# A hybrid GLA and Fourier diffusion step on one core: earlier copies of the folded h, one modulation half on TensorE, 12 Fourier units in the output gates

## The chip, the cores and the metric

The kernel runs as one launch on one core of a Trainium2 chip. The metric is the device time of a launch in microseconds (us). The profile names the engines PE (TensorE, with PEld for its weight loads), DVE (VectorE), ACT (ScalarE), POOL (GpSimd) and SP (SyncE, which here only issues transfers). All arithmetic is float32. PE gets its products at that precision by splitting each operand in a high part (a rounded copy) and a low part (the rest), and adding three products: high x high, high x low, low x high.

## The reference

There are 384 tokens (128 context, 256 latent) of width 2048, and one layer. Cut to what matters:

```python
mod = silu(cond) @ w_ada + b_ada            # six rows of 2048: sh1 sc1 ga1 sh2 sc2 ga2
h = rmsnorm(x) * (1 + sc1) + sh1
q, k, v, g, lr_f, lr_b, fo = split(h @ w_in)
o = rms(gla_forward(q, k, v) + gla_backward(q, k, v)) * silu(g)
f = fft2(fo, axes=(position, channel of a group)).real
g_a, g_b = split(sigmoid(h @ w_gate + b_gate))
m = (g_a * (o @ w_br_gla) + g_b * (f @ w_br_four)) @ w_out
x = x + ga1 * rmsnorm(m)
h = rmsnorm(x) * (1 + sc2) + sh2
x = x + ga2 * rmsnorm((silu(h @ w_ffn_gate) * (h @ w_ffn_up)) @ w_ffn_down)
```

Outputs are x of both token groups and the final GLA states.

## The kernel before, in words

Everything is held transposed: 128 channels on the partitions, the 384 tokens along the free axis. The order of PE, ACT, DVE and POOL is the order in which the program is written; SP's is set by a scheduler. A 512 KB weight goes through `load` (a transfer into a tile `raw`) and `split` (ACT rounds it to `whi`, DVE subtracts to `wlo`); `grab` takes a split weight that is ready and splits the one that comes next, so that DVE and ACT run about three weights ahead of PE. `proj` makes one 128 x 384 output from two weights, a half of 24 matmuls each, and calls a side generator behind each half.

The stages, in order:
- **Modulated input, v, q, k, decay.** h is built (tiles `A_hi`, `A_lo`), v and the other columns of w_in are projected.
- **Merge gates with GLA beside them.** 25 of the 32 column blocks of w_gate; the results go to DRAM (`gates_d`).
- **Folding** (`run_after`, 14 turns). A turn is one projection half of the last seven gate blocks, and a table `after` lists what follows it. `ends(n)` adds h's parts (`t`) and forms sums and differences of mirrored positions (`r`, `over_ends`); `parts(n)`, one turn later, splits r into high and low (`hF`, `over_parts`); `f` multiplies hF by a weight of w_in that was itself folded (`fold_across`, L248 and L249), on PE at L998 and L999 (`pfo`). Turns 2 to 9 have one such product, turns 10 to 13 two. In this stage up to five weights are loaded ahead (`depth`), three of them into extra tiles `raw3`.
- **Output gates with the transform beside them.** Eight blocks `("o", i)` of w_in; `gcol` transposes GLA's output (`pt`), applies the gate (`gs`) and splits it. The side generator runs the rest of the Fourier transform (`dft`), which reads a table of constants `cd` (L1051).
- **Merge.** Sixteen `("a", i)` blocks of w_br_gla, with the gates and the Fourier results read back from DRAM. Sixteen Fourier units (`four`, L1185 and L1186: 33 matmuls with a weight of w_br_four, then sums, a gate, and a store to `four_d`) are spread over these two stages by `mix_order`, `BF` of them among the output gates.
- **Output projection** (`wout`), with the norm's sums beside it, and then the **feed-forward** part.

Rows three to five of the modulation (m = 2, 3, 4, in two halves each) are made in the background by `ada_rest`: 16 steps per half, each of which loads 512 KB of w_ada (`adaw`, on POOL's queue) and adds it, scaled by the conditioning of each token group, to `adacc` on DVE (L679, two operations per step). Eight small matmuls (L687) and two transposes finish a half. `next(ada)` makes one step; the list of places where it stands, and the factor `rate[0]` in the output projection, spread the steps.

Of the kernel before, what the change touches and what calls it, by code (L numbers as in the profile page):

```python
# [11 lines left out]
F32 = mybir.dt.float32  # L12
# [8 lines left out]
P = 128  # L21
# [15 lines left out]
G = 1024  # L37
XU = 2
GF = 25
BF = 10  # L40
GD = 256


# [64 lines left out]
def tile_step(ctx: ExitStack, tc: tile.TileContext, a, o):  # L108
# [77 lines left out]
        mix_order += [("o", i)] + [("b", next(fourier)) for _ in range(BF * (i - 1) // 6 - BF * (i - 2) // 6)]  # L186
    for i in range(KT):
        mix_order.append(("a", i))
        if i in (1, 2, 4, 6, 8, 10):
            mix_order.append(("b", next(fourier)))  # L190
    folded = set()
    for b, i in mix_order:
# [25 lines left out]
    def load(raw=None):  # L218
        n, src = next(srcs, (0, None))
        if src is not None:  # L220
            spare = spare_raws.pop() if raw is None and spare_raws else None
            if spare:
                raw = spare.tile([P, G], F32, tag="raw3", name="raw3", bufs=3)
            elif raw is None:
                raw = wp.tile([P, G], F32, tag="raw", name="raw", bufs=2)
            dst = raw if len(src.shape) == 2 else raw.rearrange("p (n x) -> p n x", n=src.shape[1])
            SP.dma_start(dst, src)
            raws.append((raw, 1 if n in folded else 2 if n in across else 0, spare))
# [134 lines left out]
    def split_act(hi, lo, src):  # L363
        ACT.copy(hi, src)
        DVE.tensor_sub(lo, src, hi.bitcast(F32))  # L365
# [303 lines left out]
    def ada_rest(todo):  # L669
        for m, half in todo:  # L670
# [19 lines left out]
                    )  # L690
            yield from ada_tail(pr, m, half)

    def over_ends(k, t, r):

        DVE.tensor_add(t, *(x[:, k : k + 2, :].bitcast(F32) for x in hT))
        ACT.copy(r[:, :, 0 : HC + 1 : HC], t[:, :, 0 : TC + 1 : TC])
        for lo, n, e in ((0, TC, 0), (TC, TL, HC)):
            h, o = n // 2, HT + (0 if lo == 0 else HC - 2)
            hi = lo + n - 1
            DVE.tensor_add(r[:, :, e + 1 : e + 1 + h], t[:, :, lo + 1 : lo + 1 + h], t[:, :, hi : hi - h : -1])  # L700
            DVE.tensor_sub(r[:, :, o : o + h - 1], t[:, :, lo + 1 : lo + h], t[:, :, hi : hi - h + 1 : -1])

    def over_parts(k, r):

        x = hF[k // 4]
        split_act(*(x[:, k % 4 : k % 4 + 2, n, :] for n in range(2)), r)


    gates_d = dram.tile([32, P, T], F32, name="gates_d")
# [4 lines left out]
        return qk[:, h:8:4, t * P : (t + 1) * P]  # L714

    rate = [1.0]
    ada_gen = ada_rest([(m, half) for m in (2, 3, 4) for half in range(2)])
    ada = paced(ada_gen, rate)
    with ExitStack() as s:
        pg = s.enter_context(tc.tile_pool(name="pg", bufs=1))  # L720
# [243 lines left out]
    def nyq_load(eng, h):  # L964
        for g in range(4):
            src = a["w_br_four"][8 * h : 8 * h + 8, 32 * g : 32 * g + 1, (2 * g + 1) * P : (2 * g + 2) * P]
            eng.dma_start(
                wr[g : g + 65 : 32, :].rearrange("p (i c) -> p i c", c=P),
                src.rearrange("i p c -> p i c").to_broadcast([3, 8, P]),
            )  # L970

    nyq_load(POOL, 0)
    with ExitStack() as s:
        more = s.enter_context(tc.tile_pool(name="more", bufs=1))
        hF = [actp.tile([P, 4, 2, T], F32R, tag=t, name="hF") for t in ("C_lo", "B_hi", "B_lo")]
        hF.append(more.tile([P, 4, 2, T], F32R, tag="hF", name="hF"))
        spare_raws.extend([more] * 3)
        depth[0] = 5
        sums, folds = [], {}

        def ends(n):
            t, r = (more.tile([P, 2, T], F32, tag=z, name=z) for z in ("t", "r"))
            over_ends(2 * n, t, r)
            folds[n] = r

        def across_n(h, n):
            if n == 0:
                sums[:] = [pss.tile([P, 2, hi - lo], F32, tag="side", name="pfo") for _ in range(2) for lo, hi, _ in parts]
            w = take()
            push()  # L990
            w_of = [x.rearrange("p (g i k c) -> p i k g c", g=2, i=2, k=2) for x in w]
            for k in range(2):
                kt = 2 * n + k
                x = hF[kt // 4][:, kt % 4]
                for g in range(2):
                    for i, (lo, hi, _) in enumerate(parts):
                        p = sums[2 * g + i]
                        PE.matmul(p, w_of[0][:, i, k, g, :], x[:, :, lo:hi], start=kt == 0, stop=False)  # L998
                        PE.matmul(p[:, 0], w_of[1][:, i, k, g, :], x[:, 0, lo:hi], start=False, stop=kt == KT - 1)  # L999
            if n == 7:  # L1000
                for g in range(2):
                    X.append(px.tile([P, T], F32, tag="yb", name="X", bufs=4))
                    for i, (lo, hi, _) in enumerate(parts):
                        p = sums[2 * g + i]
                        ACT.copy(X[-1][:, lo:hi], p[:, 1])
                        DVE.tensor_add(X[-1][:, lo:hi], X[-1][:, lo:hi], p[:, 0])

        def run_after():
            for at, todo in enumerate(after):
                for what, *n in todo:  # L1010
                    if what == "ends":
                        ends(*n)
                    elif what == "parts":
                        over_parts(2 * n[0], folds.pop(n[0]))
                    else:
                        if n == [1, 5]:
                            depth[0] = 2
                            spare_raws.clear()
                        across_n(*n)
                if at in (0, 1, 11, 13):  # L1020
                    next(ada, None)
                yield

        ra = run_after()
        for i in range(GF, 32):
            proj(psm, hT, gate(more, i), ra)
        catch_up()
        depth[0] = 0
        xq = px.tile([P, HT], F32, name="xq")
        POOL.memset(xq, 0.0)  # L1030
        qb = pss.tile([P, HT], F32, tag="side", name="pfq")
        for kb in range(0, KT, 4):
            for x_ in range(2):
                for k in range(kb, kb + 4):
                    q = 32 * (k % 4)
                    PE.matmul(
                        qb[q : q + 4, :], wq[:, k, :], hF[k // 4][:, k % 4, x_, 0:HT].bitcast(F32),
                        start=kb == 0 and x_ == 0, stop=kb == KT - 4 and x_ == 1,
                    )
        for q in range(0, P, 32):  # L1040
            ACT.copy(xq[q : q + 4, :], qb[q : q + 4, :])
# [3 lines left out]
    with ExitStack() as s:  # L1045
# [1 line left out]
        fold_in.append(pc)  # L1047
        pw = 448
        d2 = pc.tile([P, 2 * pw], F32R, name="d2")
        cd = pc.tile([P, NC - C_CE], F32, name="cd")  # L1050
        SP.dma_start(cd, a["consts"][:, C_CE:NC])  # L1051
        table = lambda at, n, rows=P: cd[0:rows, at - C_CE : at - C_CE + n]


# [60 lines left out]
        def nyq_weights():  # L1115

            n = D // 2
            for h in range(2):
                if h:
                    nyq_load(SP, 1)  # L1120
                    yield
                    yield
                w = wn[:, n * h : n * h + n]
                ACT.copy(w, wr)
                DVE.tensor_sub(w[32:64], wr[32:64], w[32:64].bitcast(F32))
                yield

        df = dft()

        nw = nyq_weights()  # L1130

        def side():
            while True:
                next(ada, None)
                next(df, None)
                next(nw, None)
                yield
# [66 lines left out]
        for b, i in mix_order:  # L1204
            if b == "o":
                if i == 1:
                    gate_of()
                proj(psm, hT, lambda p, i=i: gcol(p, i), sd)
                if i == 1:
                    gate_of()  # L1210
                continue
            if b == "b":
                for g in (df, nw):
                    for _ in g:
                        pass
                four(i)
            else:
                catch_up()
                if mT is None:
                    mT = alloc_A()  # L1220
                if i >= KT - 6:
                    next(ada, None)
                p = psm.tile([P, T], F32, tag="mm", name="pmm")
                gemm(p, grab(hold=True), oT, 8)
                g, y = gates.pop((b, i))
                DVE.tensor_mul(g, g, p)
                DVE.tensor_add(y, y, g)
                settle()
                if late:
                    split_act(*late.pop())  # L1230
                late.append((mT[0][:, i, :], mT[1][:, i, :], y))
            gate_of()
# [7 lines left out]
    with ExitStack() as s:  # L1240
# [42 lines left out]
            ACT.activation(sq2, mg32(i), AF.Square)  # L1283
            return sq0, pr, sq2

        rate[0] = 0.75
        spare_h = {-4: ((pe, "hid_hi", 1), (pe, "hid_lo", 1)), -2: ((pe, "S0", 1), (pe, "S1", 1))}
        spare_w = ((adap, "adaw", 2), (adap, "adaw", 2))
        raw2 = None
# [739 lines left out]
```

## Time and profile before

| | |
|---|---|
| median of 3 runs | 2001.15 us (2001.08 to 2002.13) |
| the profiled execution | 1999.59 us, of which its span is 1997.8 us |
| PE busy | 1936.2 us (97%) |
| DVE busy | 1672.1 us (84%) |
| ACT busy | 916.4 us (46%) |
| mean granted TensorE clock | 0.989 |

The times in rows are us from the start of the span. By the trace the folding runs from about 441 to 567, the output gates from 570 to 699, the merge from there to 797, the output projection to 927. A row of a group gives line, engine, operation, output<-inputs, count, then busy time and mean ns. A row of the timeline gives start, length, and in brackets the idle time before it and what ended it. L998 is line 998 of the kernel before.

### The profile page before, as it was taken

What the parts mean: (1) busy time and instruction counts of PE and PEld (TensorE: products, weight loads), DVE (VectorE), ACT (ScalarE), POOL (GpSimd) and SP (SyncE); (2) the same over time, 40 slices, a digit from 0 to 9 for tenths busy, and PEclk for the clock granted to TensorE, in tenths of its full rate; (3) what the DMA queues carried; (4) which work ended last, traced back from release to release, by engine and by line L of the source; (5) the groups of instructions that cost most, each with busy time, mean ns of one, the idle gap of its engine ahead of it and who ended that gap; (6) DMA issues with size and microseconds to landing.
All of it is one profiled execution on the core that took longest, in us unless ns stands there. A gap on an engine that the chain in (4) does not pass through costs nothing.

```text
span 1997.8 us, 27420 instructions
## 1 busy us (share of the span) xinstructions
PE 1936.2 (97%) x10454; PEld 1703.6 (85%) x10454; DVE 1672.1 (84%) x2192; ACT 916.4 (46%) x1298; POOL 86.1 (4%) x154
## 2 busy tenths in 40 slices
PE   8998999997999899999999999999999999999997
PEld 6778999997889798999988888888888888888886
DVE  5668798887867998897788998999899899987885
ACT  4234445442435554446545444454444444444444
POOL 0001110101000000002100000000000000000001
PEclk9999999998999999999999999999999999999999
DMA  9975766765555787554626353544546363625243
GB/s 391 383 266 194 245 229 229 241 222 177 161 172 169 248 270 278 192 208 171 209 90 211 116 179 121 184 157 144 171 142 200 104 201 116 204 75 190 76 171 113
DMA packets 200616, 380.52 MB, mean 190 GB/s; under 512 B 14197, under 2 KB 126933, under 8 KB 196133
## 3 DMA queue, kind: packets, MB, share of 16 engines
q1 hardware_dynamic: 186004, 328.12, 48.3%
q0 software_dynamic: 13952, 50.39, 8.2%
q8 instruction: 82, 1.34, 0.3%
q14 instruction: 50, 0.40, 0.1%
q10 hardware_dynamic: 528, 0.26, 0.0%
HBM read 361.94 MB, written 16.78 MB: 190 GB/s over the span
## 4 chain that ended last, share of the span: by engine, by line
PE 78%; DVE 9%; DMA 5%; issue 4%; ACT 3%; POOL 0%; SPq 0%; DVEq 0%; ACTq 0%; POOLq 0%
PE pgu L327 30%; PE pmm L315 19%; PE pdn L327 17%; PE pv L477 3%; DVE wlo L276 2%; DVE adacc L679 2%; PE pgm L460 1%; DMA raw<-in_w_in 1%; DMA raw<-in_w_br_gla 1%; PE pmm L1446 1%; PE pfo L998 1%; PE pf L1185 1%; DMA slab<-in_w_ada 1%; PE ptr L1738 1%; DMA adaw<-in_w_ada 1%
## 5 line engine op out<-in xcount | busy, mean ns | idle before, releaser
L315 PE MATMUL pmm<-A_hi,whi 128*128 128x384 f32 x1072 | 364.2, 340 | 5.4 <-ACT gs L1147 3.1
L315 PE MATMUL pmm<-A_lo,whi 128*128 128x384 f32 x1072 | 360.6, 336 | 1.9 <-DVE A_lo L365 1.9
L315 PE MATMUL pmm<-A_hi,wlo 128*128 128x384 f32 x1072 | 360.2, 336 | 0.0
L1593 ACT CAST whi<-u 128x1024 fp32r<-128x1024 f32 x200 | 211.2, 1056 | 270.5 <-DVE u L1577 86.4
L1593 ACT CAST whi<-raw 128x1024 fp32r<-128x1024 f32 x175 | 184.5, 1054 | 213.1 <-DMA raw<-in_w_g 69.1
L1604 DVE TENSOR_TENSOR wlo<-u,whi 128x1024 fp32r<-128x1024 f32 x200 | 244.5, 1223 | 27.9 <-ACT whi L1593 16.2
L275 ACT CAST whi<-raw 128x1024 fp32r<-128x1024 f32 x165 | 173.4, 1053 | 172.0 <-DMA raw<-in_w_gate 54.2
L327 PE MATMUL pgu<-whi,A_hi 128*128 128x512 f32 x640 | 250.0, 391 | 0.0
L327 PE MATMUL pgu<-whi,A_lo 128*128 128x512 f32 x640 | 249.3, 389 | 0.0
L1604 DVE TENSOR_TENSOR wlo<-raw,whi 128x1024 fp32r<-128x1024 f32 x175 | 213.8, 1222 | 33.3 <-ACT whi L1593 21.9
L276 DVE TENSOR_TENSOR wlo<-raw,whi 128x1024 fp32r<-128x1024 f32 x163 | 198.6, 1222 | 46.9 <-ACT whi L275 46.6
L679 DVE SCALAR_TENSOR_TENSOR adacc<-adaw,spad,adacc 128x1024 f32<-128x1024 f32 x180 | 223.0, 1281 | 5.6 <-DMA adaw<-in_w_ada 5.4
L315 PEld LDWEIGHTS pmm<-A_hi,whi 128*128 128x128 f32 x1072 | 202.9, 189 | 9.1 <-ACT gs L1147 3.6
L315 PEld LDWEIGHTS pmm<-A_lo,whi 128*128 128x128 f32 x1072 | 203.0, 189 | 2.6 <-DVE A_lo L365 2.4
L315 PEld LDWEIGHTS pmm<-A_hi,wlo 128*128 128x128 f32 x1072 | 202.6, 189 | 0.0
L327 PE MATMUL pdn<-whi,hid_hi 128*128 128x512 f32 x480 | 186.9, 389 | 0.0
L327 PE MATMUL pdn<-whi,hid_lo 128*128 128x512 f32 x480 | 186.8, 389 | 0.0
L327 PE MATMUL pgu<-wlo,A_hi 128*128 128x512 f32 x640 | 184.2, 389 | 0.0
L327 PEld LDWEIGHTS pgu<-whi,A_hi 128*128 128x128 f32 x640 | 120.1, 188 | 26.0 <-issue 0.8
L327 PEld LDWEIGHTS pgu<-wlo,A_hi 128*128 128x128 f32 x640 | 120.2, 188 | 25.3
L327 PEld LDWEIGHTS pgu<-whi,A_lo 128*128 128x128 f32 x640 | 120.2, 188 | 25.0
L327 PE MATMUL pgu<-whi,S 128*128 128x512 f32 x480 | 131.1, 395 | 0.0
(402 smaller groups left out, 3047.5 us busy)
## 6 DMA issues: line engine op xcount, KB each, us to landing
adaw<-in_w_ada POOLq DMA_DIRECT2D x96, 512.0 KB, 3.9
raw<-in_w_d SPq DMA_DIRECT2D x88, 512.0 KB, 4.3
slab<-in_w_ada SPq DMA_DIRECT2D x32, 1024.0 KB, 10.0
raw<-in_w_gate SPq DMA_DIRECT2D x64, 512.0 KB, 4.7
raw<-in_w_g SPq DMA_DIRECT2D x48, 512.0 KB, 3.8
raw<-in_w_u SPq DMA_DIRECT2D x48, 512.0 KB, 4.0
raw<-in_w_in SPq DMA_DIRECT2D x44, 512.0 KB, 4.6
u<-in_w_u SPq DMA_DIRECT2D x40, 512.0 KB, 4.6
```

The costliest lines, as they stand in the source:

```text
L275: ACT.copy(hi, raw)
L276: sub = lambda: eng.tensor_sub(lo, raw, hi.bitcast(F32))
L315: PE.matmul(dst, w[wi][:, k * n + n0 : k * n + n0 + P], x[xi][:, k0 + k, :], start=first and k == 0 and j == 0, stop=last and k == kts - 1 ...
L327: PE.matmul(dst, stat[x_][m], mov(w[w_], m), start=first and w_ == m == x_ == 0, stop=last and w_ == m == 1,)
L460: PE.matmul(pgv[q : q + 32, :], spad[:, k, :], slab[k // (KT // 2)][:, k % (KT // 2), :], start=k < 4, stop=k >= KT - 4,)
L477: PE.matmul(pv[2 * t + g], hT[x_][:, kb, t * P : (t + 1) * P], w_[:, g * 512 : (g + 1) * 512], start=kb == 0 and j == 0, stop=kb == KT - 1 ...
L679: DVE.scalar_tensor_tensor(acc[:, c, :], w, spad[:, k, c : c + 1], acc[:, c, :], op0=ALU.mult, op1=ALU.add,)
L998: PE.matmul(p, w_of[0][:, i, k, g, :], x[:, :, lo:hi], start=kt == 0, stop=False)
L1185: PE.matmul(pf[:, 0 : 2 * HT], w[0][:, c], x[k], start=k == 0, stop=False)
L1446: PE.matmul(hp[u], hw[u][j][:, ((k - 1) % 8) * P : ((k - 1) % 8 + 1) * P], h2[m][:, k - 1, :], start=k == 1 and j == m == 0, stop=k == KT ...
L1593: ACT.copy(hi, src)
L1604: DVE.tensor_sub(lo, src, hi.bitcast(F32))
```

## The change

1. *Folding.* The high part of hF is copied by ACT inside `ends(n)`, right behind r; `parts(n)` keeps only DVE's subtraction.
2. *Modulation.* Half (4, 1) leaves `ada_rest` and is made by a new generator `ada_gemv`: for each of the 16 loads of w_ada, four matmuls of the conditioning (32 columns) with 256 columns of the load each. It runs from the side generator of the output gates, and its end from the first two merge blocks; `ada_rest` no longer runs there. In the folding `ada_rest` makes one step in place of four, in the merge five (blocks 9 to 13) in place of six (blocks 10 to 15), and the factor in the output projection goes from 0.75 to 0.82.
3. *Fourier units.* 12 in place of 10 stand in the output gates, two behind each of blocks 2 to 7; four in place of six in the merge, behind blocks 1, 4, 7 and 9.
4. *The table* `cd` moves into a tile that exists from the start of the folding, and its transfer is issued there in turn 7. In exchange the folding has two extra weight tiles and a depth of four.

```diff
-BF = 10
+BF = 12
...
-        if i in (1, 2, 4, 6, 8, 10):
+        if i in (1, 4, 7, 9):
...
-                raw = spare.tile([P, G], F32, tag="raw3", name="raw3", bufs=3)
+                raw = spare.tile([P, G], F32, tag="raw3", name="raw3", bufs=2)
...
+    def ada_gemv(m, half):
+
+        pr = pss.tile([P, 256], F32, tag="side", name="pr")
+        for k in range(KT):
+            w = adap.tile([P, 1024], F32, tag="adaw", name="adaw", bufs=2)
+            POOL.dma_start(w, a["w_ada"][m - 2, half, k])
+            for j in range(4):
+                PE.matmul(
+                    pr[32 * j : 32 * j + 32, :], spad[:, k, :], w[:, j * 256 : (j + 1) * 256],
+                    start=k == 0, stop=k == KT - 1,
+                )
+            yield
+        yield from ada_tail(pr, m, half)
...
-    def over_parts(k, r):
-
-        x = hF[k // 4]
-        split_act(*(x[:, k % 4 : k % 4 + 2, n, :] for n in range(2)), r)
+    def over_parts(k, r, low):
+
+        hi, lo = (hF[k // 4][:, k % 4 : k % 4 + 2, n, :] for n in range(2))
+        if low:
+            DVE.tensor_sub(lo, r, hi.bitcast(F32))
+        else:
+            ACT.copy(hi, r)
...
-    ada_gen = ada_rest([(m, half) for m in (2, 3, 4) for half in range(2)])
+    ada_gen = ada_rest([(m, half) for m in (2, 3, 4) for half in range(2)][:5])
...
+    cd = px.tile([P, NC - C_CE], F32, name="cd")
...
-        spare_raws.extend([more] * 3)
-        depth[0] = 5
+        spare_raws.extend([more] * 2)
+        depth[0] = 4
...
             over_ends(2 * n, t, r)
+            over_parts(2 * n, r, False)
...
-                        over_parts(2 * n[0], folds.pop(n[0]))
+                        over_parts(2 * n[0], folds.pop(n[0]), True)
...
-                if at in (0, 1, 11, 13):
+                if at == turns // 2:
+                    SP.dma_start(cd, a["consts"][:, C_CE:NC])
+                if at == turns - 1:
                     next(ada, None)
...
-        cd = pc.tile([P, NC - C_CE], F32, name="cd")
-        SP.dma_start(cd, a["consts"][:, C_CE:NC])
...
+        summed = ada_gemv(4, 1)
...
-                next(ada, None)
+                next(summed, None)
                 next(df, None)
...
-                if i >= KT - 6:
+                if i < 2:
+                    next(summed, None)
+                if KT - 7 <= i < KT - 2:
                     next(ada, None)
...
-        rate[0] = 0.75
+        rate[0] = 0.82
```

How the rows move on ACT, in one turn of the folding (`r` are the sums, `wq` and the first `whi` belong to the folded weight, `gz` is a gate block's eviction, the last `whi` the next gate weight). Before:

```order
L696 COPY r<-t 128x2x2
L251 COPY wq<-raw_4521 128x2x2
L281 COPY whi<-raw_4521 128x1024
L944 ACTIVATE gz<-pmm,bgate 128x384
L364 COPY hF<-r 128x2x384
L275 COPY whi<-raw 128x1024
```

Now, with the line numbers of the changed kernel:

```order
L710 COPY r<-t 128x2x2
L723 COPY hF<-r 128x2x384
L251 COPY wq<-raw 128x2x2
L281 COPY whi<-raw 128x1024
L961 ACTIVATE gz<-pmm,bgate 128x384
L275 COPY whi<-raw 128x1024
```

hF's high part stands three places earlier, ahead of the work on the folded weight.

On DVE, at the folding's start (`wlo` is a weight's low part, the row with hF its low part, the rows with r the sums). Before:

```order
L679 TENSOR_SCALAR adacc<-adaw,spad,adacc 128x1024 x2
L282 TENSOR_TENSOR wlo<-raw_4517,whi 128x1024
L276 TENSOR_TENSOR wlo<-raw_4519,whi 128x1024
L365 TENSOR_TENSOR hF<-r,hF 128x2x384
L695 TENSOR_TENSOR t<-A_hi,A_lo 128x768
L700 TENSOR_TENSOR r<-t 128x2x64
L701 TENSOR_TENSOR r<-t 128x2x63
L700 TENSOR_TENSOR r<-t 128x2x128
L701 TENSOR_TENSOR r<-t 128x2x127
L679 TENSOR_SCALAR adacc<-adaw,spad,adacc 128x1024 x2
L248 TENSOR_TENSOR raw_4521<-raw_4521 128x2x256
```

Now:

```order
L282 TENSOR_TENSOR wlo<-raw_4518,whi 128x1024
L276 TENSOR_TENSOR wlo<-raw_4520,whi 128x1024
L721 TENSOR_TENSOR hF<-r,hF 128x2x384
L709 TENSOR_TENSOR t<-A_hi,A_lo 128x768
L714 TENSOR_TENSOR r<-t 128x2x64
L715 TENSOR_TENSOR r<-t 128x2x63
L714 TENSOR_TENSOR r<-t 128x2x128
L715 TENSOR_TENSOR r<-t 128x2x127
L248 TENSOR_TENSOR raw<-raw 128x2x256
```

The two pairs of modulation steps are gone from between the folding's own rows.

On PE, in the output gates, where a block's second half ends (`pmm` is the projection, `pt` the transposes of `gcol`, `pf` a Fourier unit). Before:

```order
L315 MATMUL pmm<-A_hi,whi 128x384
L315 MATMUL pmm<-A_lo,whi 128x384
L315 MATMUL pmm<-A_hi,wlo 128x384
L1145 MATMUL pt<-ident,qk 128x128 x3
L1185 MATMUL pf<-edT,whi 128x388
L1186 MATMUL pf<-edT,wlo 128x194
```

Now:

```order
L315 MATMUL pmm<-A_hi,whi 128x384
L315 MATMUL pmm<-A_lo,whi 128x384
L315 MATMUL pmm<-A_hi,wlo 128x384
L700 MATMUL pr<-adaw,spad 32x256 x4
L1165 MATMUL pt<-ident,qk 128x128 x3
L1205 MATMUL pf<-edT,whi 128x388
L1206 MATMUL pf<-edT,wlo 128x194
```

A gemv step of four matmuls stands behind every half, 16 in all.

## The prediction

> "Faster" and "slower" below mean by more than 0.2% (4.0 us), about what a measurement of this kernel can tell from no change.
>
> **What bounds the kernel now.** I read the page first, then PE's waits, then the stages.
>
> ```profile
> span 1997.8 us, 27420 instructions
> PE 1936.2 (97%) x10454; PEld 1703.6 (85%) x10454; DVE 1672.1 (84%) x2192; ACT 916.4 (46%) x1298; POOL 86.1 (4%) x154
> ```
>
> TensorE (PE) has work for 97% of the span. The change can win only where PE waits, and everything it adds to PE is paid in full. The waits on PE (total, times, longest):
>
> ```profile
> PE pfo L998 <- DVE hF L365: 12.0, 5, 7.9
> PE pmm L315 <- ACT gs L1147: 5.4, 3, 2.3
> PE pf L1186 <- DVE wlo L276: 5.3, 5, 1.5
> PE pfo L999 <- DVE wlo L282: 4.3, 7, 0.7
> PE pp L1083 <- DMA cd<-in_consts: 3.0, 1, 3.0
> PE pmm L315 <- DVE gate L1226: 2.3, 1, 2.3
> ```
>
> The folding owns rows one and four, the transform's table row five, the output gates rows two and three, the merge the last. The stages (stretch, length, then busy time and count of PE, PEld, DVE, ACT, POOL, then PE's granted clock, DMA share, GB/s):
>
> ```profile
> 471.00:532.00 61.00, 51.74 (x281) 48.23 (x281) 45.28 (x68) 23.67 (x39) 0.80 (x2) 0.94 0.40 127
> 578.00:587.00 9.00, 9.00 (x43) 9.00 (x44) 4.31 (x6) 2.63 (x4) 0.00 (x0) 0.68 0.43 166
> 641.00:711.00 70.00, 59.94 (x339) 56.66 (x337) 63.57 (x105) 37.37 (x54) 4.24 (x8) 0.95 0.72 242
> 711.00:779.00 68.00, 67.30 (x403) 66.53 (x402) 62.73 (x112) 34.27 (x60) 1.59 (x3) 1.00 0.82 274
> 802.00:897.00 95.00, 95.00 (x560) 94.38 (x555) 85.56 (x103) 43.50 (x69) 7.42 (x14) 1.00 0.61 209
> ```
>
> In the output gates (third row) VectorE (DVE) is busy 63.57 of 70 us and PE is not; in the output projection (last row) PE has no gap.
>
> **Folding: h copied behind its sums, three of four accumulations gone.** One turn on DVE and ScalarE (ACT) (start, length, idle before):
>
> ```profile
> 480.68 0.69 DVE L248 TENSOR_TENSOR raw<-raw 128x512 f32<-128x512 f32 x1
> 484.01 0.96 DVE L365 TENSOR_TENSOR hF<-r,hF 128x768 fp32r<-128x768 f32 x1 [1.91 <-ACT hF L364]
> 489.22 0.69 DVE L248 TENSOR_TENSOR raw<-raw 128x512 f32<-128x512 f32 x1
> 482.19 1.05 ACT L281 CAST whi<-raw 128x1024 fp32r<-128x1024 f32 x1 [0.58 <-DVE raw L249]
> 483.15 0.83 ACT L364 CAST hF<-r 128x768 fp32r<-128x768 f32 x1
> ```
>
> A turn is 489.22 - 480.68 = 8.54 us, of which DVE waits 1.91 for a copy that stands behind the weight's rounding on ACT, although its input r was ready before 480.68. Put right behind r, the copy ends during L248 and L249 and that wait goes. What is late next is the weight's rounding (1.05 us and its start, against 0.96 for hF's low part): about 0.25 us. So DVE's turn becomes 8.54 - 1.91 + 0.25 = 6.9 us. PE's own turn comes from three turns with nothing waiting:
>
> ```profile
> 532.60 4.19 PE pmm L315 x24
> 541.35 4.21 PE pmm L315 x24
> 467.37 0.69 PE L998 MATMUL pfo<-hF,whi 128*128 128x388 f32 x1 [7.93 <-DVE hF L365]
> 532.43 0.36 PE L315 MATMUL pmm<-A_hi,whi 128*128 128x384 f32 x1
> 461.69 2.48 DVE L679 SCALAR_TENSOR_TENSOR adacc<-adaw,spad,adacc 128x1024 f32<-128x1024 f32 x2 [1.55 <-DMA adaw<-in_w_ada]
> ```
>
> Between the first two rows lie one projection half (4.19) and two Fourier products, so a product is 2.28 and a turn with one is 6.47 us. From 467.37 - 7.93 = 459.44 to 532.43 PE does 8 products and 7 halves, 47.6 us of work, in 73.0: an excess of 25.4. In front, DVE waited 1.55 us for a modulation weight and accumulated for 2.48; without these the first product starts about 3.4 us earlier (hF's low part then waits for the second weight's rounding on ACT), at 464.0. Seven turns of 6.9 follow, then 1.4 for the last weight's low part (0.25 of wait and the 1.22 of the row below, overlapping a little) and 2.2 of products: 515.9 instead of 532.43, **-16.5**. Bounds: -6 if the turn stays as it is (3.4 and the other early accumulation, 2.5); with PE setting the pace 464.0 + 2.28 + 7 x 6.47 = 511.6, of which some 2 us are lost to a clock lowered by the first wait (as behind the table, below), so -19. The turns with two products cost 8.75 on PE either way. Prefetch falls from five weights to four, two per turn: a load still has over a turn to land, more than the 4.6 us that one takes.
>
> ```profile
> raw<-in_w_in SPq DMA_DIRECT2D x44, 512.0 KB, 4.6
> L276 DVE TENSOR_TENSOR wlo<-raw,whi 128x1024 fp32r<-128x1024 f32 x163 | 198.6, 1222 | 46.9 <-ACT whi L275 46.6
> ```
>
> **The table during folding.**
>
> ```profile
> 577.77 0.77 PE L1083 MATMUL pp<-cd,X 128*128 128x129 f32 x2 [2.97 <-DMA cd<-in_consts]
> 586.66 0.33 PE L1098 MATMUL pe<-cd,yq 128*128 128x194 f32 x1
> 595.28 0.38 PE L1083 MATMUL pp<-cd,X 128*128 128x129 f32 x1
> 601.32 0.49 PE L1098 MATMUL pe<-cd,yq 128*128 128x194 f32 x2
> ```
>
> From the wait's start (574.80) to 586.66 PE takes 11.86 us for what it does in 6.04 the second time (595.28 to 601.32): 2.97 of wait, and 2.85 because the clock then stood at 0.68 (second stage row). With the table there early both go: **-5.8**. Lower bound -3.0, the wait alone, if another input is just as late. Its DMA goes out on SyncE's queue behind the first two folded weights, so they are not delayed.
> The Trainium skill ("TensorE: Matmul & The Clock Gate", the HAM clock gate) has the clock fall to half only after about 3.4 us without work. By that this wait cost 2.97 and no more, and the sum would be 2.9 us smaller; the 0.68 right behind it disagrees, so the measurement decides.
>
> **Output gates: accumulations out, gemv in, two more Fourier units.** The accumulations leave 16 times two of this row from DVE:
>
> ```profile
> L679 DVE SCALAR_TENSOR_TENSOR adacc<-adaw,spad,adacc 128x1024 f32<-128x1024 f32 x27 | 33.5, 1279 | 0.0
> 627.24 0.49 PE L1145 MATMUL pt<-ident,qk 128*128 128x128 f32 x3
> 640.74 0.49 PE L1145 MATMUL pt<-ident,qk 128*128 128x128 f32 x3
> 632.53 8.37 PE pmm L315 x48
> 698.75 0.44 PE L315 MATMUL pmm<-o_hi,whi 128*128 128x384 f32 x1 [2.27 <-ACT gs L1147]
> 682.28 0.61 DVE L1148 SCALAR_TENSOR_TENSOR gs<-gs,gnorm,pt 128x384 f32<-128x384 f32 x1
> 700.92 0.61 DVE L1148 SCALAR_TENSOR_TENSOR gs<-gs,gnorm,pt 128x384 f32<-128x384 f32 x1
> ```
>
> A gate unit with two Fourier units takes PE 13.50 us when nothing waits (627.24 to 640.74): 8.37 of projection, 5.13 for the transposes and 2 x 2.44. On DVE such a unit takes 18.64 (last two rows). From 640.74 to 698.75 PE has three and a half units less one Fourier unit, 3 x 13.50 + 5.13 - 2.44 = 43.2 us, and takes 58.0: 14.8 of excess. Without four accumulations a unit is 18.64 - 4 x 1.24 = 13.7 us on DVE, and on PE 13.50 plus two gemv steps. So PE leads by about a microsecond per unit; with so little slack I count 11.5 of the 14.8 as recovered: **-11.5** (bounds 0 and -16.5, with the first two merge units that inherit DVE's lag). The two moved Fourier units cost PE the same in either place, and DVE has each unit's room for them. The loads rise from 242 GB/s to some 270 (58.0 us of that stretch become about 51); the merge ran at 274 with PE busy 67.30 of 68 (fourth stage row).
>
> Each gemv step is 4 matmuls of 32 weight columns. The nearest rows:
>
> ```profile
> 614.87 1.07 PE L687 MATMUL pr<-adacc,selr 128*32 128x256 f32 x16
> 615.87 0.55 PE L1145 MATMUL pt<-ident,qk 128*128 128x128 f32 x3
> 61.19 0.83 PE L502 MATMUL px<-scr,wlr 128*32 128x384 f32 x8
> 61.94 1.66 PE L477 MATMUL pv<-whi,A_hi 128*128 128x512 f32 x6
> ```
>
> Eight such matmuls (two records each) hold PE for 1.00 us, four wider ones for 0.75. I take 0.65 for a step, 10.4 for 16, less 1.1 for the eight that go: **+9.3** (bounds +7 at 0.5 a step, +15 at 1.0). Nothing on PE's queue can pass a step, so a late weight would hold up everything; but a step's load starts when the step two before it ends, some 14 us ahead.
>
> **The rest.** The last merge units now carry five accumulation steps, not six, and the last Fourier unit comes one merge unit earlier: **-1** (bounds +4, -4). The output projection takes two more steps, 4.8 us of DVE in a stage with 9.4 us free: **0** (bound +3).
>
> **Sum**: -16.5 - 5.8 - 11.5 + 9.3 - 1 = -25.5. The profiled execution took 1999.6, so 1974.1; the runs' median stands 1.6 above it, which gives 1975.7. I say **1975**.
>
> **Rivals.**
> - *Each step pays for changing the array's shape* (chance 0.11). The row for is that eight matmuls take 1.00 us and four wider ones 0.75, so part of it is fixed; if all of it is, a step costs 1.0: 1975 + 5.6 = 1981. The Trainium skill ("TensorEngine Tiling (Array Packing)", Key Properties) says that changing the tiling mode drains TensorE, which speaks against 32 such changes; no row shows it alone.
> - *The folding's turn stays at 8.5* (0.12), because something else, such as four buffers, holds DVE: -6 in place of -16.5, 1986.
> - *Loads set the pace of the output gates* (0.17). Four weights per unit go through two buffers, so a buffer's cycle is half a unit: landing (4.6 us), 1.05 for rounding, 1.22 for the low part. At 14.8 there are 5 us for landing. For it: the DMA share is 0.72 already. Against it: the merge's 274 GB/s without a stall. Each microsecond per unit costs 6; at 17.5 the kernel takes 1991 (0.09 for up to there and somewhat beyond), and from 19.1 per unit, a landing of 7.3 us, it is no faster; at 20.5 it takes 2009, **slower** (0.08).
> - *The waits come back elsewhere and nothing is gained* (0.05): the merge or the projection, with DVE at 85.56 of 95 us, gives back what the earlier stages won; about 2001.
>
> **Numbers.** The forecast has 0.55. Faster: 0.55 + 0.11 + 0.12 + 0.09 = 0.87; same 0.05; slower 0.08. Range 1964 (folding at PE's pace, all of the output gates' excess, cheap steps) to 1991 (second rival with dear steps, or 17.5 per unit).
>
> **What would show it.** Right: no wait of hF's low part on its copy; L998's waits under 5 us in all; turns of 6.9; no wait on cd and a clock near 1 behind it; gate units near 14.8; DVE's accumulation count down by 32 in 1672.1 us; a step near 0.65. Wrong: turns of 8.5, waits of the new matmuls on adaw, or ACT's rounding waiting for raw in the output gates.

## The result, and the profile after

The changed kernel takes **1973.16 us** (median of 4 runs, 1972.12 to 1976.35) beside 2001.12 for the kernel before (4 runs, 1998.26 to 2002.13): a ratio of 0.9865, 95% interval 0.9848 to 0.9882. The forecast was 1975 in 1964 to 1991. The total is met, but two of its terms are badly off and cancel. The medians moved by 28.0 us. The profiled runs took 1999.59 and 1976.35 (the slowest of the four); their spans differ by 23.3, and what is read from the traces below adds up to that. In the order of the prediction, the page first:

```profile
span 1974.5 us, 27637 instructions
PE 1935.3 (98%) x10566; PEld 1699.0 (86%) x10566; DVE 1637.8 (83%) x2160; ACT 914.5 (46%) x1298; POOL 85.7 (4%) x154
```

PE is as busy as before (1935.3 us, 1936.2 then) in a span 23.3 us shorter, and DVE has the 32 instructions fewer. PE's waits in the stages that changed (total, times, longest; line numbers here are those of the changed kernel, and further down those of the kernel shown):

```profile
PE pmm L315 <- ACT gs L1167: 5.8, 4, 2.3
PE pfo L1017 <- DVE hF L721: 4.2, 1, 4.2
PE ptm L657 <- ACT adev L653: 2.8, 2, 2.3
PE pr L687 <- DVE adacc L679: 1.1, 2, 0.6
PE pfo L1018 <- DVE wlo L282: 0.5, 2, 0.3
```

Gone are the waits of the Fourier units (`pf`) on `wlo`, of the transform on its table, of the merge on its gate. The folding's are down from 16.3 us to 4.7, nearly all of it in front of its first product. Kept, and slightly larger, is the one on `gs` in the output gates, and the one of the modulation's last transposes (`ptm`) has grown from 1.0. Folding and table on PE's timeline (start, length, wait before in brackets): the first product, the projection behind the eighth one (f7), the Nyquist products that follow the folding, the first transform matmul, the second transform set.

```profile
463.11 0.42 PE L1017 MATMUL pfo<-hF,whi 128*128 128x388 f32 x1 [4.20 <-DVE hF L721]
513.42 0.36 PE L315 MATMUL pmm<-A_hi,whi 128*128 128x384 f32 x1
548.63 0.68 PE L1057 MATMUL pfq<-hF,wq 128*4 128x194 f32 x12
556.32 0.49 PE L1102 MATMUL pp<-cd,X 128*128 128x129 f32 x2
563.04 0.60 PE L1117 MATMUL pe<-cd,yq 128*128 128x194 f32 x2
```

The first product came at 463.11 (forecast 464.0), the end of f7 at 513.42 (515.9; 532.43 before): **-19.0**. Of this 0.5 was there before the folding began: the last wait-free stretch ahead of it starts on PE at 437.91, before at 438.45, in the same code. Turns on DVE (the low parts), and the copy that was moved:

```profile
466.27 0.95 DVE L721 TENSOR_TENSOR hF<-r,hF 128x768 fp32r<-128x768 f32 x1
473.47 0.95 DVE L721 TENSOR_TENSOR hF<-r,hF 128x768 fp32r<-128x768 f32 x1
480.39 0.95 DVE L721 TENSOR_TENSOR hF<-r,hF 128x768 fp32r<-128x768 f32 x1
487.61 0.95 DVE L721 TENSOR_TENSOR hF<-r,hF 128x768 fp32r<-128x768 f32 x1
```

```profile
472.31 0.84 ACT L723 CAST hF<-r 128x768 fp32r<-128x768 f32 x1 [1.00 <-DVE r L715]
```

The copy ends before DVE wants it, and no low part waits. The turns are 6.92 and 7.2 us by turns, 7.07 on average (466.27 to 508.67 for six); only the first, from 462.01, is shorter, 4.26. From the Nyquist products to the second transform set PE took 563.04 - 548.63 = 14.41 us, of which two gemv steps are 1.14: 13.3 beside 19.04 before (567.62, where these products began then, to 586.66), so **-5.8** as forecast.

Now the output gates. A unit is one block of the gates with the Fourier units and side steps in it. The transposes that open a unit, and the merge's first Fourier product:

```profile
594.22 0.55 PE L1165 MATMUL pt<-ident,qk 128*128 128x128 f32 x3
609.25 0.55 PE L1165 MATMUL pt<-ident,qk 128*128 128x128 f32 x3
624.28 0.55 PE L1165 MATMUL pt<-ident,qk 128*128 128x128 f32 x3
640.04 0.55 PE L1165 MATMUL pt<-ident,qk 128*128 128x128 f32 x3
659.14 0.55 PE L1165 MATMUL pt<-ident,qk 128*128 128x128 f32 x3
675.43 0.55 PE L1165 MATMUL pt<-ident,qk 128*128 128x128 f32 x3
695.45 0.34 PE L1205 MATMUL pf<-edT,whi 128*128 128x388 f32 x1
```

Two units of 15.03, then 15.76, 19.10, 16.29 and 20.02 with the first merge unit: forecast was 14.8 throughout. ACT says why. This is one cycle, DVE and ACT in order of time:

```profile
638.70 0.68 DVE L237 TENSOR_TENSOR ws<-raw 128x512 f32<-128x512 f32 x1
649.33 0.35 DVE L1210 TENSOR_TENSOR fd<-fd,pf 128x194 f32<-128x194 f32 x1
656.25 0.69 DVE L237 TENSOR_TENSOR ws<-raw 128x512 f32<-128x512 f32 x1
```

```profile
644.78 1.05 ACT L275 CAST whi<-raw 128x1024 fp32r<-128x1024 f32 x1 [3.31 <-DMA raw<-in_w_in]
645.85 1.28 ACT L1167 ACT_TABLE_LOAD   x1
647.14 0.49 ACT L1167 ACTIVATE gs<-pmm 128x384 f32<-128x384 f32 x1
648.31 0.51 ACT L364 CAST o_hi<-gs 128x384 fp32r<-128x384 f32 x1 [0.68 <-DVE gs L1168]
```

A Fourier weight's folding ends at 639.38 and frees a raw buffer; a weight is in it for ACT at 644.78, 5.4 us later. Its rounding stands on ACT ahead of the gate's Silu (647.14, with a table load of 1.28 us between the two), that ahead of the copies of the Fourier sums, and DVE's sums (from 649.33) ahead of the next foldings; the one in the same place of the next unit starts its second half 17.55 us after the first row above. The loop closes over two buffers and three queues (loads, ACT, DVE). It is the prediction's third rival, in half of the stage: "ACT's rounding waiting for raw in the output gates" was on its list of signs. ACT's waits for raw from 594 to 700 us (total, times, longest):

```profile
ACT whi L275 <- DMA raw<-in_w_in: 9.9, 3, 3.6
ACT whi L275 <- DMA raw<-in_w_br_gla: 8.2, 3, 3.1
```

PE shows them as its wait on `gs` (5.8 us), and in one more place: the transposes that finish the new half of the modulation wait for ACT's copy of its sums, which stands behind rounding and gates.

```profile
689.59 0.69 PE L657 MATMUL ptm<-ident,adev 128*128 128x128 f32 x2 [2.30 <-ACT adev L653]
```

Behind the longer of these waits PE's clock reads 0.50 from 648.3 to 651.7 us and again from 689.3 to 692.7.

What a gemv step costs, between two projection halves:

```profile
603.72 0.64 PE L700 MATMUL pr<-adaw,spad 128*32 128x256 f32 x8
604.29 0.45 PE L315 MATMUL pmm<-A_hi,whi 128*128 128x384 f32 x1
```

From its start to the next matmul 0.57 us. But a unit with two steps takes 15.03 and one without 13.50 (640.74 - 627.24 before), 0.76 a step: about 0.19 more lies in its neighbours, and the whole is 16 x 0.76 less 1.0 for the matmuls that go, **+11.2**.

At the end of the output projection, where the accumulations that are left are done at once, PE waits for the last one. Below its two rows stand two short stretches (length, busy time and count of PE, PEld, DVE, ACT, POOL, PE's clock, DMA share, GB/s): three waits in 3 us, of 0.59, 0.56 and 0.49, with PE busy 1.44, and then 3.4 us at a clock of 0.50:

```profile
874.51 0.64 PE L687 MATMUL pr<-adacc,selr 128*32 128x256 f32 x8 [0.59 <-DVE adacc L679]
876.84 0.56 PE L657 MATMUL ptm<-ident,adev 128*128 128x128 f32 x2 [0.49 <-ACT adev L653]
```

```profile
874.00:877.00 3.00, 1.44 (x17) 0.48 (x18) 3.00 (x4) 2.18 (x6) 0.00 (x0) 1.00 0.48 175
877.00:880.40 3.40, 3.40 (x13) 3.40 (x13) 3.30 (x9) 0.73 (x1) 0.00 (x0) 0.50 0.85 281
```

### The profile page after: what moved, and what is told of

Its sections match the earlier page's. It is cut to its first block, busy times and chain, and to the rows that moved or that the text cites. A ratio compares the mean times of both kernels' runs of the same rounds, so it can differ in the third digit from the quotient of the medians.

```text
span 1974.5 us, 27637 instructions
## 1 busy us (share of the span) xinstructions
PE 1935.3 (98%) x10566; PEld 1699.0 (86%) x10566; DVE 1637.8 (83%) x2160; ACT 914.5 (46%) x1298; POOL 85.7 (4%) x154
## 4 chain that ended last, share of the span: by engine, by line
PE 80%; DVE 9%; DMA 5%; ACT 3%; issue 3%; SPq 0%; POOL 0%; DVEq 0%; ACTq 0%; POOLq 0%
PE pgu L327 30%; PE pmm L315 21%; PE pdn L327 17%; PE pv L477 3%; DVE adacc L679 2%; DVE wlo L276 1%; DMA raw<-in_w_in 1%; PE pgm L460 1%; PE pmm L1468 1%; PE pf L1205 1%; PE pfo L1017 1%; DMA slab<-in_w_ada 1%; PE ptr L1760 1%; DMA xraw<-in_w_x 1%; ACT whi L275 0%
## 5 line engine op out<-in xcount | busy, mean ns | idle before, releaser
L679 DVE SCALAR_TENSOR_TENSOR adacc<-adaw,spad,adacc 128x1024 f32<-128x1024 f32 x150 | 185.8, 1281 | 1.6 <-DMA adaw<-in_w_ada 1.3
```

The costliest lines, as they stand in the source:

```text
L679: DVE.scalar_tensor_tensor(acc[:, c, :], w, spad[:, k, c : c + 1], acc[:, c, :], op0=ALU.mult, op1=ALU.add,)
```

## Experiments

Ratios are to the kernel before, measured beside each; its median stood between 1998.8 and 2002.3. Differences of medians below can therefore be off by a few us, and the ratio is given where that matters. In the edits, `...` stands for lines left out, and the comments explain.

| kernel | us | ratio, 95% interval |
|---|---|---|
| changed kernel | 1973.16 | 0.9865 (0.9848-0.9882) |
| fold_only | 1986.41 | 0.9925 (0.9912-0.9939) |
| acc_only | 1992.96 | 0.9968 (0.9957-0.9980) |
| table_late | 1977.19 | 0.9889 (0.9870-0.9907) |
| bf10 | 1974.01 | 0.9859 (0.9844-0.9873) |
| dve_mod | 1979.00 | 0.9892 (0.9874-0.9910) |
| third_dve | 1971.81 | 0.9862 (0.9844-0.9879) |
| steps_at_end | 1974.50 | 0.9877 (0.9859-0.9895) |
| third_buffer | 1964.37 | 0.9813 (0.9799-0.9826) |
| third_rate | 1962.93 | 0.9817 (0.9798-0.9837) |
| third_pair | 1959.35 | 0.9805 (0.9789-0.9821) |

**third_buffer: a third raw buffer in output gates and merge.**

```diff
...
+        spare_raws.append((pc, 1))                    # ahead of the gates
+        depth[0] = 3                                  # two again from merge unit 11
...
-                g = pm.tile([P, T], F32, tag="gate", name="gate", bufs=4)
+                g = pm.tile([P, T], F32, tag="gate", name="gate", bufs=3)
...
-                y = pc.tile([P, 2, 2, P], F32, tag="hr" if m else "ht", name="yq")
+                y = pc.tile([P, 2, 2, P], F32, tag="ht", name="yq")
```

> The changed kernel with a third buffer for raw weights from the output gates to the merge (room for it comes from one gate buffer and one small transform buffer less). Theory A (two buffers close a loop: a Fourier weight's folding on DVE frees a buffer, the load lands 5.4 us later, ACT rounds it ahead of the gate's Silu, and the next folding stands on DVE behind that gate and the Fourier unit's sums, 17.5 us in all): ACT's waits for raw go, gate units fall from about 17 to 15.0-15.6 us, some 9 of the 12 us of excess go: 1964 (1962 to 1967). Theory B (the memory system is full in this stage): more loads in flight land later, units stay near 17: 1971 to 1975.

It took 1964.37. Two neighbouring units, then its row for the whole stretch from the third unit's transposes to the merge's first Fourier product, and the same stretch of the changed kernel:

```profile
656.69 0.55 PE L1165 MATMUL pt<-ident,qk 128*128 128x128 f32 x3
671.72 0.55 PE L1165 MATMUL pt<-ident,qk 128*128 128x128 f32 x3
```

```profile
596.50:685.50 89.00, 89.00 (x596) 82.29 (x593) 71.53 (x147) 55.23 (x85) 5.80 (x11) 1.00 0.82 272
```

```profile
594.20:695.40 101.20, 93.07 (x596) 85.18 (x593) 72.81 (x148) 56.64 (x87) 5.80 (x11) 0.97 0.76 246
```

Every unit takes 15.03 and PE has no gap: the same 596 matmuls in 89.0 us, not 101.2. ACT no longer waits for raw in it. The memory moved 272 GB/s, so it was not full at 246: theory A. It also gives the clean length of the stretch (without a wait or a lowered clock), so the profiled run of the changed kernel still loses 12.3 us in it: 8.1 without work on PE (5.8 and 2.3 in the waits above), and most of the rest at the lower clock. The medians differ by only 8.8, the traces by 12.9, since that run was the slowest of its four. The kernel before lost 16.5: 14.8 as the prediction counted, and 1.65 in its first merge unit.

**dve_mod and third_dve: all six halves accumulated on DVE, with two and with three buffers.**

```diff
-    ada_gen = ada_rest([(m, half) for m in (2, 3, 4) for half in range(2)][:5])
+    ada_gen = ada_rest([(m, half) for m in (2, 3, 4) for half in range(2)])
...
-                if at == turns - 1:                   # folding
+                if at >= turns - 4:
...
-                next(summed, None)                    # side of the output gates
+                next(ada, None)
...
-                if KT - 7 <= i < KT - 2:              # merge
+                if i >= KT - 6:
```

> The changed kernel with all six modulation halves accumulated on DVE again (no 32-column matmuls); four accumulation steps stand in the folding's last turns and six in the merge. By the prediction's terms (+11.5 for the gates, -9.3 for the steps, +1): 1976. Theory A (what the half on TensorE buys is mostly eaten by the loads' pace, yet DVE at 18.6 a unit is worse than 17, and the merge inherits its lag): +4, 1975 to 1979. Theory B (the loads set the pace with or without it): the steps' 9.1 us come back, 1963 to 1967.

> The kernel of third_buffer with all six modulation halves accumulated on DVE, as in dve_mod. Theory A (with accumulations DVE's 18.6 us per gate unit set the pace, and the third buffer can't help it): no better than dve_mod, 1976 to 1980, so the half on TensorE is worth some 12 to 15 with three buffers and 6 with two. Theory B (loads were all that held the gates): units at PE's 13.9, steps' 9.1 us saved: 1955 to 1960.

1979.00 and 1971.81. The first agrees with theory A (and, 3 us over, nearly as well with the prediction's terms), the second with neither theory. The same stretch of both, dve_mod first:

```profile
591.00:692.40 101.40, 87.00 (x516) 82.54 (x513) 89.58 (x162) 53.84 (x83) 5.27 (x10) 0.98 0.68 227
```

```profile
591.60:693.00 101.40, 88.40 (x516) 82.62 (x513) 89.60 (x162) 53.29 (x83) 5.28 (x10) 0.98 0.65 227
```

Both take 101.4 us, as long as the changed kernel's 101.2: with accumulations DVE sets the pace (89.6 us busy) and a third buffer shortens nothing there: PE's waits on `gs`, 7.4 us in dve_mod, are gone in third_dve, but it waits 9.2 for DVE's `wlo` where dve_mod waits 6.7; without them, with two buffers, the loads set one just as slow. What the third buffer brings in third_dve (7.2 us by the medians, 4.5 in the traces) comes elsewhere: the merge, from its first Fourier product to the next modulation reduction, takes 87.6 us in dve_mod and 82.8 in third_dve. dve_mod waits 3.35 us in it for A_lo, third_dve 0.24:

```profile
773.03 0.45 PE L315 MATMUL pmm<-A_lo,whi 128*128 128x384 f32 x1 [3.35 <-DVE A_lo L365]
```

```profile
770.39 0.44 PE L315 MATMUL pmm<-A_lo,whi 128*128 128x384 f32 x1 [0.24 <-DVE A_lo L365]
```

That the merge, too, lives on the buffers was in no theory. The half on TensorE is worth 5.8 us with two buffers and 7.4 with three by the medians, 5 and 10 by the ratios.

**bf10: the two Fourier units back in the merge.**

```diff
-BF = 12
+BF = 10
...
-        if i in (1, 4, 7, 9):
+        if i in (1, 2, 4, 6, 8, 10):
```

> The changed kernel with 10 Fourier units in the output gates and 6 in the merge, as before the change. The prediction had the two moved units at nothing: 1973. Theory A (the loop of two buffers paces gate units with two Fourier units at 17, PE needs 15.0): two units fewer pay the excess of 2 each: 1969. Theory B (the merge has no room on DVE for two more, its stalls come back): 1975 to 1978.

1974.01: the median can't be told from the changed kernel's, as the prediction's zero had it. The one profiled execution (span 1969.5, the fastest of its four) lost 5 us in the gates, not 12, and 3 in the merge, not 1. That looks like theory A, but it sets the fastest run of one kernel beside the slowest of the other, so theory A is not shown. What the loop costs differs between executions.

**steps_at_end: the merge's five accumulation steps in its last five units.**

```diff
-                if KT - 7 <= i < KT - 2:
+                if i >= KT - 5:
```

> The changed kernel with its five accumulation steps of the merge in the last five units (the change has them end two units earlier). Theory A (the accumulations behind the last units made the merge's end wait on DVE's gate and A_lo before the change, 4 to 6 us): the waits come back, 1976 to 1979. Theory B (the merge won because the gates hand on no lag of DVE): stays at 1973.

1974.50, with an interval that overlaps the changed kernel's. In the trace the wait of theory A is back:

```profile
769.78 0.52 PE L315 MATMUL pmm<-A_lo,whi 128*128 128x384 f32 x1 [3.36 <-DVE A_lo L365]
```

The unit with it takes 12.67 and the next 9.30 where 8.32 is clean: 5.3 us. But this execution lost 4 us less in the gates than the changed kernel's, and the two came to their first merge reduction at the same time (784.93 and 785.05 us). The place of the steps is shown by the trace, and its price not by the time.

**fold_only and acc_only: the folding in two parts**, each on the kernel before.

```diff
+            over_parts(2 * n, r, False)               # fold_only: rounded copy behind the sums
...
-                        over_parts(2 * n[0], folds.pop(n[0]))
+                        over_parts(2 * n[0], folds.pop(n[0]), True)
```

```diff
-                if at in (0, 1, 11, 13):              # acc_only
+                if at in (10, 11, 12, 13):
```

> The kernel before with one edit: the rounded copy of folded h is issued right behind its sums; accumulations, buffers, table and modulation as before. Theory A (DVE's wait on that copy set the turn): turns of 6.5 to 7.0, the late first product and the accumulations at turns 0 and 1 stay (3.4 and 2.5 us): about -13, 1988 (1985 to 1991). Theory B (the accumulations that the change took out of the folding carry most of it): turns stay near 8.5, -1 to -4, 1997 to 2000.

> The kernel before with one edit: the folding's accumulation steps stand in its last four turns, none in its first two. The copy of folded h stays behind the weight's rounding. The prediction's lower bound: the first product 3.4 us earlier and 2.5 from the second turn, turns of 8.5: -6, 1993 to 1995. Rival (DVE and the loads make up for it, since the turns are paced by the copy anyway and the last turns now carry two steps more): 1997 to 2001.

1986.41 and 1992.96: theory A, and the prediction's lower bound (-6.1). The Nyquist products began at 553.85 and 561.25, 13.8 and 6.4 earlier than before, together 20.1 beside the 19.0 of both. Counted from PE's last wait-free stretch ahead of the folding (438.45 before, 436.88 and 438.64 here), it is 12.2 and 6.6, together 18.8 beside 18.5. Two low parts in fold_only, which prefetches five weights, stand 6.93 apart, and its turns, too, are 6.93 and 7.2 by turns, as with the changed kernel's four; so the turn owes nothing to that number (the second rival):

```profile
478.72 0.95 DVE L707 TENSOR_TENSOR hF<-r,hF 128x768 fp32r<-128x768 f32 x1
485.65 0.95 DVE L707 TENSOR_TENSOR hF<-r,hF 128x768 fp32r<-128x768 f32 x1
```

**table_late: the table loaded behind the folding again, in the changed kernel.**

```diff
-    cd = px.tile([P, NC - C_CE], F32, name="cd")
...
-                if at == turns // 2:
-                    SP.dma_start(cd, a["consts"][:, C_CE:NC])
...
+        cd = pc.tile([P, NC - C_CE], F32, name="cd")
+        SP.dma_start(cd, a["consts"][:, C_CE:NC])
```

> The changed kernel with the transform's table loaded behind the folding again, as before the change. By the prediction's term (wait 2.97 and a lowered clock 2.85): +5.8, 1979. Theory A (with a faster folding the table's landing is met earlier: fold_only waited 6.1 us for it and took 8.5 more than the changed kernel from the Nyquist products to the second transform set): +8.5, 1981 to 1982. Theory B (the output gates' loads get ahead meanwhile and give part of it back): 1975 to 1977.

1977.19, +4.0. From the Nyquist products to the second transform set the trace has 17.4 us without its steps, 4.1 more than the changed kernel. A gemv step now stands in the wait and covers part of it, which no theory had. The first transform matmul behind three such waits, and the stretch from there to the second set (PE's clock is the figure behind the five engines), for table_late, fold_only and acc_only:

```profile
559.60 0.46 PE L1101 MATMUL pp<-cd,X 128*128 128x129 f32 x2 [2.44 <-DMA cd<-in_consts]
```

```profile
559.60:568.00 8.40, 8.40 (x49) 7.74 (x49) 2.77 (x4) 2.64 (x4) 0.00 (x0) 0.80 0.47 182
```

```profile
567.12 0.77 PE L1087 MATMUL pp<-cd,X 128*128 128x129 f32 x2 [6.10 <-DMA cd<-in_consts]
```

```profile
567.00:575.60 8.60, 8.48 (x41) 8.52 (x42) 3.56 (x5) 2.64 (x4) 0.00 (x0) 0.69 0.18 70
```

```profile
571.33 0.46 PE L1083 MATMUL pp<-cd,X 128*128 128x129 f32 x2 [2.90 <-DMA cd<-in_consts]
```

```profile
571.30:577.40 6.10, 6.07 (x41) 6.10 (x42) 2.91 (x5) 2.63 (x4) 0.00 (x0) 1.00 0.68 261
```

The clock read 0.80 behind 2.44 us, 0.69 behind 6.10, and 0.68 behind the 2.97 of the kernel before; behind 2.90 it stayed at 1.00. These are means over the stretches: read in shorter ones, the clock is 0.50 for about 3.4 us in table_late (560.4 to 563.7) and 1.00 behind that, and 0.50 for about 6.8 us in the kernel before (577.0 to 583.8). A wait of this size may or may not cost a second time.

**third_rate and third_pair: the better version.** The first paces the accumulations of the output projection faster, so that the last half ends before the rest is done at once; the second also takes the gemv's steps in pairs.

```diff
-        rate[0] = 0.82
+        rate[0] = 0.95
```

```diff
+            n = 0
...
-                next(summed, None)
+                if n % 2:                             # every second half
+                    next(summed, None)
+                    next(summed, None)
+                n += 1
```

> The kernel of third_buffer with the pace of the accumulations in the output projection at 0.95 a call and not 0.82, so that the last half ends some steps ahead of the point where the rest is done at once. Theory A (in third_buffer its two products there cost 1.2 us more than elsewhere): 1963. Theory B (DVE has no room for more steps early in the projection): 1965 to 1968.

> The kernel of third_rate with the modulation's steps on TensorE taken in pairs, eight matmuls behind every second projection half and none behind the others. Theory A (each change between 128-column and 32-column matmuls costs: a gate unit with two steps takes 15.03 and without 13.51, 0.76 a step, of which the step's own matmuls show 0.57): a unit with a pair takes 14.8 to 14.85, 8 pairs save about 1.6: 1961 beside third_rate's 1963. Theory B (the price goes by the matmuls alone): units stay at 15.0, 1963.

1962.93 and 1959.35. The first is within the noise of third_buffer, but its waits on PE from the gates to the feed-forward (590 to 912 us) are down to three, of 0.5, 0.4 and 0.2 us, that belong to neither change.

In third_pair a pair (eight matmuls) takes 1.00 and a unit 14.66, 0.37 less than with two single steps:

```profile
609.08 1.07 PE L700 MATMUL pr<-adaw,spad 128*32 128x256 f32 x16
610.08 0.55 PE L1169 MATMUL pt<-ident,qk 128*128 128x128 f32 x3
624.74 0.55 PE L1169 MATMUL pt<-ident,qk 128*128 128x128 f32 x3
```

Eight pairs save about 3.0 us, more than theory A's 1.6; the time moved by 3.6 (medians), but the two intervals overlap. The Trainium skill ("TensorEngine Tiling (Array Packing)", Key Properties) has a change of tiling mode drain TensorE: the trace agrees that a change costs, with 0.37 us for each pair of changes that goes. That a drain is what costs is not shown. third_pair is the fastest kernel here, 14 us under the changed one by the medians and 12 by the ratios.

## Why the prediction was right in sum

| term | forecast | in the traces |
|---|---|---|
| folding | -16.5 | -19.0 |
| table | -5.8 | -5.8 |
| output gates | -11.5 | -4.2 (16.5 lost before, 12.3 after) |
| gemv steps | +9.3 | +11.2 |
| merge | -1 | -7.0 (7.9 lost before, 0.8 after) |
| output projection | 0 | +2.5 |
| sum | -25.5 | -22.3 of the spans' -23.3 |

Of the last 1.0 us, 0.6 lies behind the projection, in code that did not change, and 0.4 comes from counting two steps at 0.57 in the table's row and at 0.76 in the gemv's. The terms missed by -2.5, 0, +7.3, +1.9, -6.0 and +2.5; that these nearly cancel is luck, not foresight. The rows for merge and projection are read from PE's timeline with a projection half at 4.17 and a merge Fourier unit at 2.39. Merge, from its first Fourier product to the next modulation reduction: before 708.77 to 801.85 for 17 halves and 6 such units, 85.2 clean; after 695.45 to 785.05 for 19 and 4, 88.8 clean. Projection, from there to the first statistics matmul: 124.5 before, 118.6 after with two halves less, so 2.5 more.

- **Folding**: the step held. The copy's wait went, the weight's rounding was next late (0.30 us), the turn came out at 7.07 on average for 6.9, acc_only gave the -6 of the other part. Mis-sized by 2.5 us were the start and the first turn: the first product came 0.9 earlier than forecast, and the first turn took 4.26, so that seven turns took 46.7 us where 48.3 were counted. The 3.6 for the last weight and products held. With that lead PE ran four turns at its own 6.48 and met DVE's pace only in the last two (7.07 and 6.93). The start is not the same in every execution: in third_buffer, with the same code, the first product came at 465.47, but 1.8 of these 2.4 us stood already ahead of the folding (439.73 beside 437.91).
- **Table**: right, as wait and clock. With it left late the changed kernel loses 4.1, between the bound of 3.0 and the forecast. The Trainium skill ("TensorE: Matmul & The Clock Gate", the HAM clock gate) has the clock fall after an idle window of about 3.4 us; that is not borne out by 2.44 us with 0.80 behind it. It also has that window run free of the kernel; that agrees with 2.90 and 2.97 us ending so differently.
- **Output gates**: here a step failed, "So PE leads by about a microsecond per unit; with so little slack I count 11.5 of the 14.8 as recovered". DVE did get the room (72.81 busy in 101.2 us). But the unit had a second pace hidden behind DVE's, the loop of loads through two buffers, 17.5 us long. The rival that named it was held unlikely for the merge's 274 GB/s without a stall. That compares throughput, and the loop is one of latency: third_buffer ran at 272 GB/s with no gap. The -4.2 is that of the slowest run; from what third_buffer gains it would be nearer -8 by the medians (16.5 less 8.8) and -6 by the ratios.
- **gemv**: a step's own time was near (0.57 for 0.65), and the first rival's price (1.0 a step) did not come, though part of what it says did: by third_pair a change of shape and back costs 0.37. About a fifth of a microsecond per step stands in the matmuls beside the step; read by the unit's length it costs 0.76.
- **Merge**: mis-sized, -7.0 for -1. Before, it waited at its end on DVE's gate and, one unit on, on A_lo, and took 6.5 us over clean in these two units; the fourth rival had such waits come, and they went. The change ends its accumulations two units earlier, and steps_at_end has the A_lo wait back. That third_dve loses it again with steps in the last units shows that the raw buffers have a part in it; how much of each was not separated.
- **Output projection**: the bound of +3 was nearer than the forecast of 0. The last accumulation and its reduction came in one go with PE waiting (1.6 us in three waits, and the clock at 0.50 behind them), and third_rate takes that away.

## What to carry to other kernels

An engine that is given room uncovers the next pace, so work out the loop through the buffers (landing, the queues between one release and the next) before counting an engine's excess as won, and weigh it as latency, not as GB/s. A price that is read from an instruction's own duration leaves out what it does to its neighbours: compare whole units with and without it. When a sum of terms is met, look at the terms: here errors of 7 and 6 us cancelled by luck, and the largest miss showed where some 9 us more could be had.

## What the hardware showed that was not expected

- A switch from 128-column to 32-column matmuls and back costs about 0.4 us on PE beyond the matmuls themselves (a unit takes 15.03 us with two single steps, 14.66 with one pair and 13.50 with none).
- Of two waits of nearly the same length, 2.97 and 2.90 us, one was followed by a clock of 0.68 (mean of 9 us) and the other by 1.00. Three waits of 0.49 to 0.59 us close together were followed by 0.50 for 3.4 us.
